# Six pairs of gate tiles computed in seven products instead of eight

## The chip, the cores and the metric

The kernel runs on one core of one Trainium2 chip. Its time is the device time of the execution in microseconds (us), as a median of three runs. A core has a matrix engine (TensorE, PE), three engines that work on rows of 128 partitions (VectorE or DVE, ScalarE or ACT, GpSimd or POOL), and DMA queues that load from memory; SyncE (SP) issues most of the loads. Each engine runs its own list of instructions in order, and semaphores make one wait for another.

## The reference

One layer of a decoder with four parallel branches (T = 512 steps, D = 1024 channels), shortened:

```python
h = rms_norm(x, mix_norm)
z = h @ w_in                                       # branches' inputs, and 4 x 1024 gate logits
y_sc, y_pool, y_conf, y_diff = ...                 # gated short conv, pooling, Conformer conv, differential attention
gates = sigmoid(gate_logits).reshape(b, s, 4, D)
merged = sum_i gates[i] * y[i]
x = x + merged @ w_o
x = x + conv_glu_ffn(rms_norm(x, ffn_norm), ffn_up, ffn_conv, ffn_down)

def conformer_conv(u, conv_w, conv_b, ln_g, ln_b, w_out):
    a, gate = split(u)
    y = causal_dwconv(a * sigmoid(gate), conv_w) + conv_b      # 31 taps, 512 channels
    y = silu(layer_norm(y, ln_g, ln_b))
    return y @ w_out
```

## The kernel before, in words

All activations lie with the channel on the partition and time along the row. Every matrix product is done in a reduced float format three times: weight and activation are both split into a high and a low part, and `mm3` (L181 to L184) issues high by high, high by low and low by high. A tile of the output is 128 channels by 512 steps and fills one of eight PSUM banks.

The weights come as a stream of chunks, 128 x 1024 each, in the order in which they are used. `fetch` loads a chunk into one of two raw buffers, `load_chunk` makes its high part on ScalarE (`wh`, L144) and its low part on VectorE (`wl`, L145); each has a ring of three buffers. A slot of the ring comes free when TensorE has used the chunk three places earlier.

TensorE goes through the stages in the order of the program: the Conformer's projections, q, k and v, the inputs of the short convolution and of pooling, and then for each branch the output projection and the gate of each of the eight tiles m: `ys`/`gts` (short convolution), `yp`/`gtp` (pooling), `yd`/`gtd` (attention). A gate tile is 8 x 3 matmuls of 512 columns on the normed input `hs`; `gate` applies the sigmoid on ScalarE, `merge` multiplies and adds on VectorE (L601, L607). The eight gates of the convolution branch (`gtc`) come next, and after them its output projection `yc`, `wo` and the feed-forward layer in two parts.

The 31 taps of the Conformer convolution for each of four channel tiles run on VectorE (`cacc`, L388 and L391) beside the matmuls of the attention, the short convolution and pooling. Between the c gates stands the layer norm: `norm_mean` (L632 to L637, ahead of gate m = 2) adds the four tiles to `cm`, splits the sum into `muh` (ScalarE) and `mul` (VectorE), and two matmuls with `ones` give the mean `mu`. The squares of the differences give `var` in the same way ahead of gate m = 4 (`norm_out`, L303 to L309), then SiLU makes the inputs of `yc`.

The last product of the feed-forward layer (`dn`) is done by a scheme with seven instead of eight block products: `seven` takes two tiles of the output and two blocks of the contraction, and multiplies sums of weight blocks with sums of activation blocks, 256 columns wide. The sums of the weights are made by DMA in memory, on the GpSimd queue (`make_sums`, L217 to L232), in 11 groups.

The order of ScalarE and VectorE is set at build time by a list scheduler that goes by its own costs; the order of GpSimd is that of the program.

Of the kernel before, what the change touches and what calls it, by code (L numbers as in the profile page):

```python
# [56 lines left out]
NTMP = 13  # L57
# [21 lines left out]
def hybrid_layer_kernel(ctx: ExitStack, tc: tile.TileContext, xT: bass.AP, w: bass.AP, cols: bass.AP, wa: bass.AP,  # L79
# [27 lines left out]
    up0 = w.shape[0] - 2 * NP  # L107
    plan = [("n", c) for c in range(up0 + 2 * CUT)]
    plan += [("s", c) for c in range(MP * CUT // 2)]
    plan += [("n", c) for c in range(up0 + 2 * CUT, w.shape[0])]  # L110
    plan += [("s", c) for c in range(MP * CUT // 2, MP * NP // 2)]
    sums = [dram.tile([P, GRP * SW], F32, name=f"sums{g}") for g in range(MP * NP // 2 // GRP)]
# [3 lines left out]
    def fetch(i, pieces=1):  # L116
        kind, c = plan[i]
        if kind == "s":
            g, o = divmod(c, GRP)
# [417 lines left out]
    def sc_in(j):  # L537
# [103 lines left out]
    def norm_out():  # L641
        rl = rsqrt(colsum(total, "var"), 1.0 / 512, t2("rl"), "rl")
        for j in range(4):
# [63 lines left out]
    def operands(i, ge, go, homes):  # L707
        def slot(name):
# [9 lines left out]
        nc.vector.scalar_tensor_tensor(  # L718
            out=wt[:, :H], in0=vt[:, :H], scalar=-1.0, in1=b22, op0=ALU.mult, op1=ALU.subtract)
        nc.vector.scalar_tensor_tensor(  # L720
            out=wt[:, H:], in0=wt[:, :H], scalar=-1.0, in1=b21, op0=ALU.mult, op1=ALU.subtract)
# [4 lines left out]
        return {"b11": (e[:, left], e[:, right]), "b22": pick(o, left), "b21": pick(o, right), "v1": pick(v, left),
                "t3": pick(v, right), "w2": pick(w_, left), "t4": pick(w_, right)}

    def seven(name, ops):
        a, b, c, d = (bank(f"{name}{x}") for x in "abcd")  # L730
        r1, r6, r2, r7, r5, r4, r3 = d[:, :H], a[:, :H], a[:, H:], b[:, :H], b[:, H:], c[:, :H], c[:, H:]
        n = len(ops)
        for k, x in enumerate(ops):
            a12, a11, a22, s3_, s1_, s2_, s4_ = blocks7()
            f, l = k == 0, k == n - 1
            mm3(r1, a11, x["b11"], f, l, True)
            mm3(r5, s1_, x["v1"], f, l, True)
            mm3(r6, s2_, x["w2"], f, l, True)
            mm3(r2, a12, x["b21"], False, l, True)
            mm3(r7, s3_, x["t3"], False, l, True)  # L740
            mm3(r4, a22, x["t4"], f, l, True)
            mm3(r3, s4_, x["b22"], False, l, True)
        s15 = t2(f"{name}s")
        s1_, s5_ = s15[:, :H], s15[:, H:]
        nc.scalar.copy(s1_, r1)
        nc.scalar.copy(s5_, r5)

        def two(x):
            return x.rearrange("p (b n) -> p b n", n=H)

        def twice(x):
            return x.unsqueeze(1).broadcast_to([P, 2, H])

        p1, p2, p3 = t2(f"{name}p"), t2(f"{name}q"), t2(f"{name}r")
        nc.vector.tensor_tensor(out=two(p1), in0=two(a), in1=twice(s1_), op=ALU.add)
        nc.vector.tensor_tensor(out=two(p2), in0=two(b), in1=twice(p1[:, :H]), op=ALU.add)
        nc.vector.tensor_tensor(out=p3, in0=c, in1=p2, op=ALU.add)
        nc.vector.tensor_tensor(out=s5_, in0=p2[:, :H], in1=s5_, op=ALU.add)
        return p1[:, H:], p3[:, H:], p3[:, :H], s5_

    parts = ((0, CUT), (CUT, NP))
    for part, (p0, p1) in enumerate(parts):
# [7 lines left out]
        for m in range(MP):  # L770
# [14 lines left out]
def _layout(x, mix_norm, w_in, sc_conv, sc_out, pool_w, pool_scale, conf_conv, conf_conv_b, conf_ln_g, conf_ln_b,  # L785
# [33 lines left out]
    for br, outs in ((0, so), (1, None), (3, do), (2, None)):  # L819
        for m in range(KD):  # L820
            if br == 2:
                tile_of(win, 36 + br * 8 + m)
                continue
            if outs is None:
                parts.append(pw[m // 2][:, (m % 2) * P:(m % 2 + 1) * P])
            else:
                tile_of(outs, m)
            tile_of(win, 36 + br * 8 + m)
# [65 lines left out]
```

## Time and profile before

| | |
|---|---|
| time, median of 3 runs | 880.69 us (880.65 to 880.88) |
| profiled execution | 880.71 us, of it 878.9 us in the span of the trace |
| granted TensorE clock, mean | 0.999 |
| busy, share of the span | PE 99%, PE weight loads 84%, DVE 75%, ACT 46%, POOL 8% |
| memory traffic | 182 GB/s over the span |

The span runs from the first to the last instruction. A busy share says how much of it an engine was at work; an engine with a low share can still be the one that is waited for in one place. Matmul records overlap, so their pace is read from one start to the next.

### The profile page before, as it was taken

The page shows a single profiled execution, that of the slowest core. Times are in us where ns is not written, and L with a number is a line of the kernel's source. Part 1 is how long each engine was busy: PE and PEld are TensorE (multiplying, and loading weights), DVE is VectorE, ACT ScalarE, POOL GpSimd, SP SyncE. Part 2 cuts the span into 40 slices and gives each one's busy share as a digit, 9 for nine tenths or more (in the row PEclk, how much of TensorE's full clock was granted, in tenths as well). Part 3 has the DMA queues.
Part 4 walks back from the last instruction along what each step waited for, and adds up shares of the span by engine and source line. Part 5 has one row for each costly group of instructions (what it writes and reads, how often), then busy time and mean ns, then how long its engine had stood idle before and what let it go on. Part 6 is the DMA issues. An engine that isn't in the chain of part 4 may idle for free.

```text
span 878.9 us, 11626 instructions
## 1 busy us (share of the span) xinstructions
PE 871.6 (99%) x4372; PEld 739.0 (84%) x4372; DVE 659.3 (75%) x1091; ACT 404.9 (46%) x636; POOL 71.3 (8%) x101
## 2 busy tenths in 40 slices
PE   9999999999999999999999999999999999999997
PEld 7888888888888888888888888888899888888997
DVE  7399966897957999534468566988886788888865
ACT  7343455464675432222564345444454344444542
POOL 1003300002411101111101100000000000000000
PEclk9999999999999999999999999999999999999999
DMA  6322242222479888888789862323662423334671
GB/s 235 114 96 97 80 123 73 72 97 97 138 200 213 183 215 206 220 216 205 189 208 250 226 157 72 119 97 103 208 178 63 131 98 97 96 106 158 174 210 49
DMA packets 54921, 128.98 MB, mean 147 GB/s; under 512 B 4896, under 2 KB 24352, under 8 KB 54688
## 3 DMA queue, kind: packets, MB, share of 16 engines
q1 hardware_dynamic: 36512, 95.98, 32.9%
q0 software_dynamic: 17776, 31.72, 18.5%
q8 instruction: 34, 0.56, 0.3%
q10 hardware_dynamic: 576, 0.53, 0.2%
q14 instruction: 23, 0.19, 0.1%
HBM read 126.12 MB, written 33.82 MB: 182 GB/s over the span
## 4 chain that ended last, share of the span: by engine, by line
PE 99%; DVE 0%; issue 0%; DVEq 0%
PE fg L182 5%; PE fu L182 5%; PE fg L183 5%; PE fu L183 5%; PE fg L184 5%; PE fu L184 5%; PE gts L182 2%; PE gts L184 2%; PE gts L183 2%; PE gtp L182 2%; PE gtc L182 2%; PE gtp L184 2%; PE gtc L183 2%; PE wo L183 2%; PE wo L182 2%; PE gtd L184 2%
## 5 line engine op out<-in xcount | busy, mean ns | idle before, releaser
L144 ACT CAST wh<-wr 128x1024 fp32r<-128x1024 f32 (+1 forms) x137 | 140.1, 1026 | 199.8 <-PE gtd L183 33.1
L145 DVE TENSOR_TENSOR wl<-wr,wh 128x1024 fp32r<-128x1024 f32 (+1 forms) x137 | 163.4, 1196 | 75.2 <-ACT wh L144 68.6
L391 DVE SCALAR_TENSOR_TENSOR cacc<-glu,colt,cacc 128x512 f32<-128x512 f32 x120 | 89.7, 752 | 1.9
L686 DVE SCALAR_TENSOR_TENSOR fc<-f,colt,fc 128x512 f32<-128x512 f32 x88 | 65.8, 749 | 7.7 <-ACT fc L684 6.4
L182 PE MATMUL fg<-hs,wh 128*128 128x512 f32 x176 | 68.5, 389 | 0.0
L184 PE MATMUL fg<-hs,wl 128*128 128x512 f32 x176 | 68.5, 389 | 0.0
L183 PE MATMUL fg<-hs,wh 128*128 128x512 f32 x176 | 68.5, 389 | 0.0
L182 PE MATMUL fu<-hs,wh 128*128 128x512 f32 x176 | 68.5, 389 | 0.0
L183 PE MATMUL fu<-hs,wh 128*128 128x512 f32 x176 | 68.5, 389 | 0.0
L184 PE MATMUL fu<-hs,wl 128*128 128x512 f32 x176 | 68.5, 389 | 0.0
L144 ACT CAST wh<-ra 128x384 fp32r<-128x384 f32 x44 | 22.6, 513 | 46.8 <-PE dn12c L183 7.6
L684 ACT ACTIVATE fc<-f,colt 128x512 f32<-128x512 f32 x44 | 31.6, 718 | 19.1 <-DVE f L103 16.6
L184 PEld LDWEIGHTS fu<-hs,wl 128*128 128x128 f32 x176 | 33.1, 188 | 6.9
L184 PEld LDWEIGHTS fg<-hs,wl 128*128 128x128 f32 x176 | 33.0, 188 | 6.9
L182 PEld LDWEIGHTS fg<-hs,wh 128*128 128x128 f32 x176 | 33.0, 188 | 6.9
L183 PEld LDWEIGHTS fg<-hs,wh 128*128 128x128 f32 x176 | 33.1, 188 | 6.8
L182 PEld LDWEIGHTS fu<-hs,wh 128*128 128x128 f32 x176 | 33.0, 188 | 6.8
L183 PEld LDWEIGHTS fu<-hs,wh 128*128 128x128 f32 x176 | 33.0, 188 | 6.8
L145 DVE TENSOR_TENSOR wl<-ra,wh 128x384 fp32r<-128x384 f32 x44 | 24.4, 554 | 19.1 <-ACT wh L144 19.0
L681 DVE TENSOR_TENSOR f<-fu,rs 128x512 f32<-128x512 f32 x22 | 15.1, 688 | 20.4 <-PE fu L184 20.4
L145 DVE TENSOR_TENSOR wl<-rb,wh 128x512 fp32r<-128x512 f32 x44 | 30.2, 687 | 0.0
L144 ACT CAST wh<-rb 128x512 fp32r<-128x512 f32 x44 | 27.1, 617 | 0.0
(1673 smaller groups left out, 2375.6 us busy)
## 6 DMA issues: line engine op xcount, KB each, us to landing
wr<-w SPq DMA_DIRECT2D x132, 512.0 KB, 3.3
sums<-s POOLq DMA_DIRECT2D x11, 1024.0 KB, 9.4
rb<-sums SPq DMA_DIRECT2D x44, 256.0 KB, 4.0
ra<-wa SPq DMA_DIRECT2D x44, 192.0 KB, 3.7
sums<-s POOLq DMA_DIRECT2D x11, 512.0 KB, 7.0
sums<-s POOLq DMA_DIRECT2D x11, 256.0 KB, 5.4
x<-xT SPq DMA_DIRECT2D x8, 256.0 KB, 5.6
xin<-xT SPq DMA_DIRECT2D x1, 1024.0 KB, 7.8
```

The lines of the kernel that those rows point to most:

```text
L144: nc.scalar.copy(hi[:, s], src)
L145: nc.vector.tensor_tensor(out=lo[:, s], in0=src, in1=hi[:, s].bitcast(F32), op=ALU.subtract)
L182: nc.tensor.matmul(ps, a[0], b[0], start=start, stop=False, skip_group_check=shared)
L183: nc.tensor.matmul(ps, a[0], b[1], start=False, stop=False, skip_group_check=shared)
L184: nc.tensor.matmul(ps, a[1], b[0], start=False, stop=stop, skip_group_check=shared)
L391: nc.vector.scalar_tensor_tensor(out=acc31[j], in0=glus[j][:, i:i + T], scalar=wc, in1=acc31[j], op0=ALU.mult, op1=ALU.add)
L681: nc.vector.tensor_tensor(out=u[:, 2:2 + T], in0=ps, in1=rs, op=ALU.mult)
L684: nc.scalar.activation(c, u[:, 2:2 + T], AF.Copy, scale=col("ffn_conv", o + 2))
L686: nc.vector.scalar_tensor_tensor(out=c, in0=u[:, i:i + T], scalar=col("ffn_conv", o + i), in1=c, op0=ALU.mult, op1=ALU.add)
```

## The change

Two pairs of gate tiles in the attention branch (m = 4, 5 and 6, 7) and all four pairs in the convolution branch go through `seven` as well. Their activation operands are sums of halves of `hs`, made once by `fold` on VectorE and ScalarE, four times. Their weights come in chunks of 128 x 896 (`wa` and sums made by DMA): four chunks for a pair. The sums now have 17 groups, the first three made early. All chunks, and the temporary of the fold, use one ring of raw buffers, which has three instead of two. `seven` issues the product r1 last in its first step. The splits of `yconf` go to the buffers of `od`.

```diff
@@ fetch, plan @@
+PLAN = [("n", 57 + 3 * STD // 2)]
+for _ in range((KD - STD) // 2):
+    PLAN += [("n", 1), ("s", FOLD)]
+PLAN += [("s", MP * FOLD), ("n", 4 + 8 + 2 * CUT), ("s", MP * CUT // 2), ("n", 2 * (NP - CUT)), ("s", MP * (NP - CUT) // 2)]
...
+        raw = wp.tile([P, CW], F32, tag="raw", name=f"wr{i}", bufs=3)
         if kind == "s":
             g, o = divmod(c, GRP)
-            ra, rb = m2(f"ra{i}", F32), m2(f"rb{i}", F32)
-            nc.sync.dma_start(ra[:, :AW], wa[c])
-            nc.sync.dma_start(rb, sums[g][:, o * SW:(o + 1) * SW])
-            return ((slice(0, AW), ra[:, :AW]), (slice(AW, AW + SW), rb))
-        raw = wp.tile([P, CW], F32, tag="raw", name=f"wr{i}", bufs=2)
+            n = AW + SW
+            nc.sync.dma_start(raw[:, :AW], wa[c])
+            nc.sync.dma_start(raw[:, AW:n], sums[g][:, o * SW:(o + 1) * SW])
+            return ((slice(0, n), raw[:, :n]),)
...
+    after(QLAG + 1, lambda: make_sums(0, EARLY))
...
-        u = padded(f"u{j}", 2)
+        u = padded(f"u{j}", 2, eng=nc.vector)
...
-    after(SUMU, make_sums)
+    after(SUMU, lambda: make_sums(EARLY, len(sums)))
...
+    def fold(i):
...
+        k = slice(2 * i, 2 * i + 2)
+        f = wp.tile([P, CW], F32, tag="raw", name=f"hf{i}", bufs=3)
+        nc.vector.tensor_tensor(
+            out=f.rearrange("p (k t) -> p k t", t=T), in0=hs[:, k, 0, :].bitcast(F32),
+            in1=hs[:, k, 1, :].bitcast(F32), op=ALU.add)
+        b12, b11, b22, b21 = (f[:, j * H:(j + 1) * H] for j in range(4))
+        vt, wt = t2(f"hv{i}"), t2(f"hw{i}")
+        nc.vector.tensor_tensor(
+            out=vt.rearrange("p (b n) -> p b n", n=H), in0=f[:, H:3 * H].rearrange("p (b n) -> p b n", n=H),
+            in1=b12.unsqueeze(1).broadcast_to([P, 2, H]), op=ALU.subtract)
+        combos(vt, wt, b11, b12, b21, b22)
+        v = split(vt, "", dst=(slot(f"hvh{i}"), slot(f"hvl{i}")))
+        w_ = split(wt, "", dst=(slot(f"hwh{i}"), slot(f"hwl{i}")))
...
+    def seven(name, ops):
...
+            if not f:
+                mm3(r1, a11, x["b11"], f, l, True)
+            mm3(r5, s1_, x["v1"], f, l, True)
...
+            mm3(r3, s4_, x["b22"], False, l, True)
+            if f:
+                mm3(r1, a11, x["b11"], f, l, True)
+        s15 = t2(f"{name}s")
+        s1_, s5_ = s15[:, :H], s15[:, H:]
+        nc.scalar.copy(s1_, r1)
+        nc.scalar.copy(s5_, r5)
...
+        nc.vector.tensor_tensor(out=two(p1), in0=two(a), in1=twice(s1_), op=ALU.add)
+        nc.vector.tensor_tensor(out=two(p2), in0=two(b), in1=twice(p1[:, :H]), op=ALU.add)
+        nc.vector.tensor_tensor(out=p3, in0=c, in1=p2, op=ALU.add)
+        nc.vector.tensor_tensor(out=s5_, in0=p2[:, :H], in1=s5_, op=ALU.add)
...
+    def gate_pair(m, name, keep=False):
+        c11, c12, n21, n22 = seven(f"g{name}{m}", hops)
+        gs = [m2(f"sg{name}{m + i}", F32) if keep else t2(f"sg{name}{m + i}") for i in range(2)]
+        for g, c, x, scale in (
+                (gs[0], right, c11, 1.0), (gs[0], left, c12, 1.0), (gs[1], right, n21, -1.0), (gs[1], left, n22, -1.0)):
+            nc.scalar.activation(g[:, c], x, AF.Sigmoid, scale=scale)
+        return gs
...
-    for m in range(KD):
+    for i in range(FOLD):
+        after(FOLDS * i, lambda i=i: fold(i))
+    for m in range(STD):
         py = mixed(m, "d", ydiff)
         merge(m, py, gate(m, "d"))
+    for m in range(STD, KD, 2):
+        pys = [mixed(m + i, "d", ydiff) for i in range(2)]
+        for i, g in enumerate(gate_pair(m, "d")):
+            merge(m + i, pys[i], g)
...
-            yconf.append(split(a, f"yc{j}"))
-
-    for m in range(KD):
+            yconf.append(split(a, "", dst=(od[0][:, j, :], od[1][:, j, :])))
+
+    for m in range(0, KD, 2):
         if m == 2:
             while events:
                 events.pop(0)[2]()
             norm_mean()
         if m == 4:
             norm_out()
-        gates.append(gate(m, "c", True))
+        gates += gate_pair(m, "c", True)
```

The built program shows what this moves. On TensorE, before the change, the two matmuls of the mean stand between two gates of 512 columns (`gtc`, tiles 1 and 2):

```order
L184 MATMUL gtc_3586<-hs,wl_3519 128x512
L322 MATMUL mu<-muh,ones 128x512
L323 MATMUL mu<-mul,ones 128x512
L182 MATMUL gtc_3659<-hs,wh_3555 128x512
L183 MATMUL gtc_3659<-hs,wh_3555 128x512
```

With the change, `gc0` and `gc2` are the first and second pair of c gates, and a to d their four banks:

```order
L189 MATMUL gc0c<-hs,wh_3810 128x256
L190 MATMUL gc0c<-hs,wh_3810 128x256
L191 MATMUL gc0c<-hs,wl_3811 128x256
L329 MATMUL mu<-muh,ones 128x512
L330 MATMUL mu<-mul,ones 128x512
L189 MATMUL gc2b<-at_111,wh_3839 128x256
L190 MATMUL gc2b<-at_111,wh_3839 128x256
```

The mean is still behind two tiles of gates, which are now one pair.

On VectorE, before the change, around the sums for the mean (`cm`, and `mul`, the low part of its split):

```order
L145 TENSOR_TENSOR wl_3519<-wr_3516,wh_3518 128x1024
L632 TENSOR_TENSOR cm<-cacc_705,cacc_1590 128x512
L601 TENSOR_TENSOR sgd_3548<-yd_3501,sgd_3548 128x512
L145 TENSOR_TENSOR wl_3556<-wr_3553,wh_3555 128x1024
L607 TENSOR_TENSOR acc_2764<-acc_2764,sgd_3548 128x512
L634 TENSOR_TENSOR cm<-cm,cacc_2626 128x512
L634 TENSOR_TENSOR cm<-cm,cacc_3285 128x512
L208 TENSOR_TENSOR mul<-cm,muh 128x512
```

With the change, on the same engine at the same place; `gc0p` to `gc0s` are the additions that end the first pair, `cacc_3367` is the Conformer's fourth channel tile:

```order
L667 TENSOR_TENSOR gc0q<-gc0b,gc0p 128x512
L398 SCALAR_TENSOR_TENSOR cacc_3367<-glu_208,colt,cacc_3367 128x512
L668 TENSOR_TENSOR gc0r<-gc0c,gc0q 128x512
L669 TENSOR_TENSOR gc0s<-gc0q,gc0s 128x256
L398 SCALAR_TENSOR_TENSOR cacc_3367<-glu_208,colt,cacc_3367 128x512
L727 TENSOR_TENSOR cm<-cacc_711,cacc_1608 128x512
L398 SCALAR_TENSOR_TENSOR cacc_3367<-glu_208,colt,cacc_3367 128x512
L729 TENSOR_TENSOR cm<-cm,cacc_2656 128x512
L398 SCALAR_TENSOR_TENSOR cacc_3367<-glu_208,colt,cacc_3367 128x512
L152 TENSOR_TENSOR wl_3955<-wr_3836,wh_3954 128x896
L729 TENSOR_TENSOR cm<-cm,cacc_3367 128x512
L215 TENSOR_TENSOR mul<-cm,muh 128x512
```

The last taps of the fourth tile and the end of the first c pair now stand ahead of `cm` and `mul`.

Where that fourth tile starts on VectorE: before the change, in the pooling branch, between the taps of the third tile (`cacc_2626`):

```order
L601 TENSOR_TENSOR acc_2764<-ys_2696,sgs_2762 128x512
L391 SCALAR_TENSOR_TENSOR cacc_2626<-glu_200,colt,cacc_2626 128x512
L388 TENSOR_SCALAR cacc_3285<-glu_202,colt 128x512
L391 SCALAR_TENSOR_TENSOR cacc_2626<-glu_200,colt,cacc_2626 128x512
L391 SCALAR_TENSOR_TENSOR cacc_3285<-glu_202,colt,cacc_3285 128x512
L391 SCALAR_TENSOR_TENSOR cacc_2626<-glu_200,colt,cacc_2626 128x512
L391 SCALAR_TENSOR_TENSOR cacc_3285<-glu_202,colt,cacc_3285 128x512
```

With the change, behind the low parts of the first 896-wide chunk and of the last fold, beside the first attention pair:

```order
L152 TENSOR_TENSOR wl_3393<-wr_3383,wh_3392 128x896
L215 TENSOR_TENSOR hwl_3364<-hw_3355,hwh_3363 128x512
L395 TENSOR_SCALAR cacc_3367<-glu_208,colt 128x512
L398 SCALAR_TENSOR_TENSOR cacc_3367<-glu_208,colt,cacc_3367 128x512 x5
L152 TENSOR_TENSOR wl_3431<-wr_3386,wh_3430 128x896
L690 TENSOR_TENSOR sgd_3421<-yd_3351,sgd_3421 128x512
L398 SCALAR_TENSOR_TENSOR cacc_3367<-glu_208,colt,cacc_3367 128x512
L696 TENSOR_TENSOR acc_2480<-acc_2480,sgd_3421 128x512
```

The first of its 31 instructions (L395, before the change L388) has moved from the pooling branch to the attention branch, behind the folds; the other 30 (L398, before L391) follow there.

## Rows read from the trace of the kernel before

**Rows 1.** Page, parts 1 and 4: busy us and share; last chain.

```profile
PE 871.6 (99%) x4372; PEld 739.0 (84%) x4372; DVE 659.3 (75%) x1091; ACT 404.9 (46%) x636; POOL 71.3 (8%) x101
...
PE 99%; DVE 0%; issue 0%; DVEq 0%
```

**Rows 2.** Stretches: length, busy us from PE to POOL, PEclk, DMA share, GB/s.

```profile
360.00:380.00 20.00, 20.00 (x90) 16.57 (x89) 6.59 (x8) 4.57 (x6) 1.61 (x2) 1.00 0.82 218
380.00:400.00 20.00, 20.00 (x90) 16.57 (x89) 8.87 (x10) 5.48 (x7) 2.98 (x4) 1.00 0.86 207
400.00:420.00 20.00, 20.00 (x90) 16.57 (x89) 9.07 (x12) 6.31 (x8) 2.88 (x4) 1.00 0.82 214
```

**Rows 3.** Timeline of VectorE: start, duration, line, operation, tiles.

```profile
355.25 0.74 DVE L391 SCALAR_TENSOR_TENSOR cacc<-glu,colt,cacc 128x512 f32<-128x512 f32 x1
...
415.64 0.69 DVE L607 TENSOR_TENSOR acc<-acc,sgd 128x512 f32<-128x512 f32 x1
416.24 1.41 DVE L634 TENSOR_TENSOR cm<-cm,cacc 128x512 f32<-128x512 f32 x2
418.34 0.69 DVE L208 TENSOR_TENSOR mul<-cm,muh 128x512 fp32r<-128x512 f32 x1 [0.68 <-ACT muh L207]
```

**Rows 4.** Timeline of TensorE at the mean.

```profile
423.23 0.39 PE L322 MATMUL mu<-muh,ones 128*128 128x512 f32 x1
```

**Rows 5.** Timeline of TensorE, start of yd4.

```profile
379.71 0.39 PE L182 MATMUL yd<-od,wh 128*128 128x512 f32 x1
379.94 0.39 PE L183 MATMUL yd<-od,wh 128*128 128x512 f32 x1
```

**Rows 6.** Timeline of TensorE in the seven products of dn.

```profile
650.43 0.28 PE L182 MATMUL dn01a<-at,wh 128*128 128x256 f32 x1
650.55 0.28 PE L183 MATMUL dn01a<-ol,wh 128*128 128x256 f32 x1
```

**Rows 7.** VectorE's lines, 340 to 480: busy us, mean ns, idle before.

```profile
L145 DVE TENSOR_TENSOR wl<-wr,wh 128x1024 fp32r<-128x1024 f32 x25 | 30.6, 1222 | 39.3 <-ACT wh L144 39.3
L391 DVE SCALAR_TENSOR_TENSOR cacc<-glu,colt,cacc 128x512 f32<-128x512 f32 x14 | 10.5, 750 | 0.3
```

**Rows 8.** Page, part 5: a low part 512 wide.

```profile
L145 DVE TENSOR_TENSOR wl<-rb,wh 128x512 fp32r<-128x512 f32 x44 | 30.2, 687 | 0.0
```

**Rows 9.** Additions ending seven: ns min/median/max, first and last start.

```profile
L755 DVE TENSOR_TENSOR dn01p<-dn01a,dn01s x1: 681/681/681, 655.9 to 655.9; 128x512 f32<-128x512 f32 x1
...
L758 DVE TENSOR_TENSOR dn01s<-dn01q,dn01s x1: 416/416/416, 658.2 to 658.2; 128x256 f32<-128x256 f32 x1
```

**Rows 10.** ScalarE's lines, 340 to 480.

```profile
L144 ACT CAST wh<-wr 128x1024 fp32r<-128x1024 f32 x26 | 27.4, 1052 | 59.5 <-PE gtd L183 33.1 <-PE gtc L183 13.9 <-PE yd L183 7.6
L646 ACT ACTIVATE cacc<-cacc,colt 128x512 f32<-128x512 f32 x4 | 3.1, 810 | 0.0
L304 ACT ACT_TABLE_LOAD x1 | 1.3, 1283 | 0.0
L207 ACT CAST muh<-cm 128x512 fp32r<-128x512 f32 x1 | 0.6, 618 | 3.8 <-DVE cm L634 3.8
```

**Rows 11.** Stretches at both ends of the span; the clock is PEclk.

```profile
0.00:4.00 4.00, 2.54 (x6) 2.07 (x7) 0.48 (x1) 1.58 (x2) 2.45 (x30) 1.00 0.43 139
...
873.00:874.00 1.00, 0.09 (x1) 0.00 (x0) 0.90 (x2) 0.00 (x0) 0.00 (x0) 1.00 0.00 0
876.00:877.00 1.00, 0.00 (x0) 0.00 (x0) 0.08 (x1) 0.00 (x0) 0.00 (x0) 0.86 1.03 345
```

**Rows 12.** Timeline of TensorE at the start.

```profile
1.46 4.64 PE L269 MATMUL warm<-zeros 128*128 128x512 f32 x10 [1.46 <-DVE zeros L266]
5.89 0.59 PE L182 MATMUL ca<-raw0h,wh 128*128 128x512 f32 x1
```

**Rows 13.** Loads, 300:480 and 560:620: KB each, us to landing.

```profile
wr<-w SPq DMA_DIRECT2D x33, 512.0 KB, 4.8
...
wr<-w SPq DMA_DIRECT2D x11, 512.0 KB, 3.3
```

More of the change, by code (lines that the diff above doesn't have):

```diff
@@ L47 @@
 SUMU = 30
+EARLY = 3
 DEEP = 2
+STD = 4
+FOLD = 4
+FOLDS = 12
+PLAN = [("n", 57 + 3 * STD // 2)]
+for _ in range((KD - STD) // 2):
+    PLAN += [("n", 1), ("s", FOLD)]
+PLAN += [("s", MP * FOLD), ("n", 4 + 8 + 2 * CUT), ("s", MP * CUT // 2), ("n", 2 * (NP - CUT)), ("s", MP * (NP - CUT) // 2)]
 LOG_EXP = "natural_log_exp_and_others"
@@ L56 @@
 SQ0 = 8
-NTMP = 13
+NTMP = 12
 SQS = 4
@@ L106, in hybrid_layer_kernel @@
     chunks = []
[L107 to L112, printed above, removed]
+    plan, n_of = [], {"n": 0, "s": 0}
+    for kind, n in PLAN:
+        plan += [(kind, n_of[kind] + i) for i in range(n)]
+        n_of[kind] += n
+    sums = [dram.tile([P, GRP * SW], F32, name=f"sums{g}") for g in range(n_of["s"] // GRP)]
     fetched = []
@@ L229, in make_sums @@
             lambda g: nc.gpsimd.dma_start(view(g, 3, 4), src(s3, g, 1), accum_op=ALU.add))
-        for g in range(len(sums)):
+        for g in range(g0, g1):
             for f in steps:
@@ L588, in hybrid_layer_kernel, with combos, table @@
     merged = []
-    after(SUMU, make_sums)
+    after(SUMU, lambda: make_sums(EARLY, len(sums)))
+    H = T // 2
+    left, right = slice(0, H), slice(H, T)
+    def combos(vt, wt, b11, b12, b21, b22):
+        nc.vector.scalar_tensor_tensor(
+            out=wt[:, :H], in0=vt[:, :H], scalar=-1.0, in1=b22, op0=ALU.mult, op1=ALU.subtract)
+        nc.vector.scalar_tensor_tensor(
+            out=wt[:, H:], in0=wt[:, :H], scalar=-1.0, in1=b21, op0=ALU.mult, op1=ALU.subtract)
+    def table(b11, b22, b21, v, w_):
+        pick = lambda x, c: (x[0][:, c], x[1][:, c])
+        return {"b11": b11, "b22": b22, "b21": b21, "v1": pick(v, left), "t3": pick(v, right),
+                "w2": pick(w_, left), "t4": pick(w_, right)}
@@ new lines, in hybrid_layer_kernel, with slot @@
+    hops = []
+    hhome = [x[:, i, :] for x in at_ for i in range(4)]
+    def fold(i):
+        def slot(name):
+            return hhome.pop(0) if hhome else m2(name)
+        k = slice(2 * i, 2 * i + 2)
[11 more added lines that the diff above has]
+        w_ = split(wt, "", dst=(slot(f"hwh{i}"), slot(f"hwl{i}")))
+        e, o = hs[:, 2 * i], hs[:, 2 * i + 1]
+        pick = lambda x, c: (x[:, 0, c], x[:, 1, c])
+        hops.append(table(pick(e, right), pick(o, left), pick(o, right), v, w_))
@@ L717, in operands @@
         nc.vector.tensor_tensor(out=vt[:, H:], in0=b22, in1=b12, op=ALU.subtract)
[L718 to L721, printed above, removed]
+        combos(vt, wt, b11, b12, b21, b22)
         v = split(vt, "", dst=(slot(f"vh{i}"), slot(f"vl{i}")))
         w_ = split(wt, "", dst=(slot(f"wh{i}"), slot(f"wl{i}")))
-        left, right = slice(0, H), slice(H, T)
         pick = lambda x, c: (x[0][:, c], x[1][:, c])
[L726 to L759, printed above, removed]
+        return table((e[:, left], e[:, right]), pick(o, left), pick(o, right), v, w_)
     parts = ((0, CUT), (CUT, NP))
@@ L818, in _layout, with gate_of @@
         tile_of(win, 12 + g)
[L819 to L828, printed above, removed]
+    def gate_of(br, m):
+        tile_of(win, 36 + br * 8 + m)
+    for m in range(KD):
+        tile_of(so, m)
+        gate_of(0, m)
+    for m in range(KD):
+        parts.append(pw[m // 2][:, (m % 2) * P:(m % 2 + 1) * P])
+        gate_of(1, m)
+    for m in range(STD):
+        tile_of(do, m)
+        gate_of(3, m)
+    for m in range(STD, KD):
+        tile_of(do, m)
     for m in range(KD):
```

29 lines of the change are left out of this document (23 added, 6 removed).

## The prediction

> **What bounds the kernel now.** I read the busy times first: TensorE is busy for 99% of the span, VectorE for 75%, and the chain that ended last is TensorE for 99% [rows 1]. So a matmul taken off shortens the kernel by its issue spacing, as long as TensorE is never kept waiting; whatever makes TensorE wait adds its full length. The question is therefore whether the covers still hold: the weight splits, and the two column sums of the Conformer's layer norm, `mu` and `var`, which TensorE meets in the middle of the c gates.
>
> The table of stretches comes next. VectorE is busy for only 6.59 us of 360 to 380, 8.87 of 380 to 400 and 9.07 of 400 to 420 [rows 2]. This idle time stands directly ahead of the c gates, and it is what let the mean be ready early: the last Conformer tap ran at 355.25, the last two `cm` sums from 416.24, `mul` at 418.34 to 419.03 [rows 3], and TensorE took `mu` at 423.23 [rows 4]. The cover was 4.2 us.
>
> **What the seven products give.** Matmuls of 512 columns start 0.227 us apart [rows 5], those of 256 columns 0.120 us apart [rows 6]. A pair of gates takes 2 x 8 x 3 = 48 wide matmuls, 48 x 0.2267 = 10.88 us; in seven products it takes 4 x 7 x 3 = 84 narrow ones, 84 x 0.1200 = 10.08 us. Six pairs save 6 x 0.80 = 4.8 us. That is all that TensorE can gain, and the kernel would then stand at 875.9.
>
> **What VectorE pays, and where.** The durations: a tap 0.750, a 1024-wide low part 1.22 [rows 7]; 512 wide 0.687 [rows 8]; a merge, which is 512 wide like `mul`, 0.69 [rows 3]. Where one doesn't need the result of the other they start some 0.09 us closer than they last: the merge at 415.64 lasts 0.69 us, and the next row starts 0.60 us later [rows 3]. A 896-wide low part therefore lies between 0.687 and 1.22; by the line through both it is 1.09, less 0.09, and I take 1.0. An epilogue of seven products is three additions 512 wide and one 256 wide, 3 x 0.68 + 0.42 = 2.5 us [rows 9].
>
> Each of the four folds is one addition 1024 wide, one subtraction 512 wide, two combinations 256 wide and two low parts: about 1.1 + 0.6 + 2 x 0.35 + 2 x 0.65 = 3.7 to 4.1 us, estimated from the same rows. The folds themselves hold no matmul up, since gd4 comes last of what follows them. But in the built order they take the place that the taps of j=3 had in the pool branch, and these 31 taps now stand beside the new gate pairs, right up to `cm`.
>
> I walk VectorE from the first of them. Ahead of it stands the low part of the first 896-wide chunk; its cast needs a slot of the ring of three, which TensorE frees at the end of yd3. In the rows, yd4 starts at 379.71 [rows 5]; 24 spacings before that is 374.27. With the cast (896 wide, between 0.62 and 1.05 us [rows 10]) and two low parts, the taps start at 376.9. From there to the end of `mul` VectorE has: 31 taps x 0.75 = 23.3; 14 low parts of 896 x 1.0 = 14.0; one of 1024, 1.1; ten merges x 0.65 = 6.5; three epilogues, 7.4; three `cm` sums, 2.0; the cast `muh` 0.62 [rows 10] and `mul` 0.69, 1.3. The sum is 55.6 us, so `mul` ends at 432.4.
>
> TensorE, from 379.71: two pairs of 5.44 + 10.08 bring it to 410.75, and gc0 ends at 420.83 if nothing waits. By the same list the low part of gc0's fourth chunk is ready 12.6 us before `mul`, at 419.9, while its third matmul is due at 418.55: **+1.4**. gc0 then ends at 422.2. TensorE takes its matmuls in order, and the two of `mu` stand directly behind gc0's last and ahead of gc2's first. It waits from 422.2 to 432.4: **+10.2**.
>
> Bounds of this wait. From below: even with VectorE free, gc0's epilogue, five taps, a low part, three sums and the split stand behind gc0's bank a, which is complete 1.08 us before gc0 ends. Epilogue 2.5 + 5 x 0.75 + 1.0 + 2.0 + 1.3 = 10.5, less 1.08 and some overlap, is 9.0 us. From above: if two late weight chunks hold VectorE up too, about 13.
>
> **What follows.** `var` stands behind gc2. Its `varh` is queued on ScalarE behind the cast of the chunk that reuses gc2's last slot and a sigmoid; its `varl` on VectorE behind that chunk's low part and the rest of gc2's epilogue. After gc2's end that is 0.9 + 0.4 + 0.6 = 1.9 us plus the latency of the handovers to `varh`, and 4.1 us to `varl`, of which eight narrow matmuls of gc4 cover 1.0: **+2.8** (1.9 to 4). Then ScalarE has two table loads of 1.28 us, four SiLU of 0.81 [rows 10], four casts and two copies ahead of the cast of gc6's third chunk. These 10.7 us begin 2.1 us before gc4's end, and the cast itself is done 7.7 us behind it at the earliest by overlapped starts; it is due after two chunks, 5.04 us: **+2.8** (1 to 4). From yc on, the order of every engine and its slack are as before; I cost that at nothing. The same goes for the other edits: TensorE's rows ahead of yd4 are those of before, the memset of `u` is four short writes, the splits of `yc` only land elsewhere, and moving the r1 product changes no count. Three early groups of sums are loads at a time when TensorE's weights come in with room; if they did delay a chunk there, 1 to 2 us would be lost.
>
> **The clock.** The granted clock was still 1.00 where the last matmul ended at about 873.1; in the stretch 876 to 877 it was 0.86 [rows 11], a mean over the two levels: 0.28 us of it at the lower, 1.2 GHz, so it fell at about 876.7. That was 3.6 us after the last matmul; I expect it to fall in a pause of 10 us and not in the short ones. The price of coming back is in the first matmuls: the ten `warm` ones, 512 wide, take from 1.46 to 5.89, where the next starts, 0.44 us each [rows 12], where 0.227 is the spacing later: 4.43 - 2.27 = **+2.2**. The clock column speaks against this, since it has 1.00 for 0 to 4 us too [rows 11]; by the column a restart costs nothing. I take the spacing, since it is what delays work.
>
> The Trainium skill, "TensorE: Matmul & The Clock Gate", Part 1 ("What's actually happening"), says that the throttled clock is the default state and that activity releases it; its note on trace caveats ("Seeing it yourself") says that the clock events of a trace are not always to be trusted. By that page the restart costs about what the spacing gives; by the column it costs 0, and the sum would be 2.2 us lower.
>
> **DMA.** A seven-product pair reads 1792 KB in place of 1024 KB. While the sums run a load of 512 KB lands after 4.8 us, against 3.3 us afterwards [rows 13]. Three raw slots, each held for about 5 us of landing and 2.1 us of splitting, give a chunk every 2.4 us against the 2.52 us that TensorE needs. This holds, but barely: I cost it at 0, with 4 as the upper end. Against a lasting shortage, TensorE's own pauses give the ring time to fill.
>
> **Sum**, against the profiled execution of 880.71 us (878.9 of span and 1.8 outside), which equals the median of 880.69: -4.8 + 1.4 + 10.2 + 2.8 + 2.8 + 2.2 = +14.6, so **895.3 us**.
>
> **Rivals.**
> 1. *The means arrive in time* (faster). If the taps of j=3 were run in the pool branch, or `mul` found a free VectorE, only the gain would be left: 875.9 us; it turns faster than before as soon as all waits together are under 4.8 us. For it: VectorE has 25 idle us between 360 and 400 [rows 2]. Against it: the taps are behind a slot that TensorE frees, the list from there is 55.6 us long, and even its last part alone is 9 us. 3 in 100; about no change, 2 in 100.
> 2. *Only the shortest wait for `mu`*: 9.0 - 4.8 and nothing further, or 2 to 3 us of the rest: 885 to 889. For it: handovers overlap more than I count, and ScalarE may run ahead. Against it: `var` is tied to gc2's end. 15 in 100.
> 3. *The late chunks decide as well*: mul at +13, contention +4 on top: 899 to 903. For it: the landing row under the sums. Against it: the pauses themselves. 15 in 100.
> 4. *The clock does not fall or comes back at once*: 893.1, within my range. 20 in 100 of the forecast's own cases.
>
> My forecast, 889 to 899 about 895.3, has 65 in 100. The range, which should hold 8 in 10, is 887 to 901. Differences under 0.2% (1.8 us) count as no change. Faster 0.03, same 0.02, slower 0.95.
>
> **What would show it.** In the profile after, TensorE's busy share is down, and its longest wait, some 10 us, is for `mul`, between gc0 and gc2; taps of line 398 run until just before it. VectorE has no pause from about 377 to 432. The spacing within the new pairs is 0.120 us, except for the first microseconds behind `mu`, where it is about twice that. There are shorter waits for `varh` and `varl`, and for gc6's third chunk. If `mu` waits for less than 5 us, my list of VectorE's work is wrong; if new waits stand before 410 or behind yc, supply and not order is the cause. If the pairs themselves take over 10.1 us with no wait, the gain was mis-sized.

## The result, and the profile after

The changed kernel takes 905.64 us (median of four, 900.72 to 908.5), the kernel before 880.67 on the same chip: ratio 1.0277 (95% interval 1.0232 to 1.0322). That is slower, as forecast, but by 25.0 us where 14.6 had been predicted, and beyond the range's upper end of 901. The profiled execution (905.76) has a span of 903.9 us, 25.0 more than before; every stage below is read from it.

The page now has TensorE busy for 97% and the last chain no longer on TensorE alone (parts 1 and 4; compare [rows 1]):

```profile
PE 874.7 (97%) x4588; PEld 750.9 (83%) x4588; DVE 694.2 (77%) x1111; ACT 420.3 (46%) x636; POOL 92.9 (10%) x121
...
PE 90%; DVE 4%; DMA 3%; ACT 2%; issue 1%; SPq 0%; DVEq 0%; ACTq 0%
```

TensorE's waits say where (what waited, for what; us in total, times, longest):

```profile
PE mu L329 <- ACT muh L214: 10.3, 1, 10.3
PE var L329 <- ACT varh L214: 5.6, 1, 5.6
PE gc6d L189 <- ACT wh L151: 2.8, 1, 2.8
PE gc0d L191 <- DVE wl L152: 1.4, 1, 1.4
PE gd6d L191 <- DVE wl L152: 0.6, 1, 0.6
PE gc0d L189 <- DVE gd6p L666: 0.5, 1, 0.5
PE gc0c L189 <- ACT gd6s L656: 0.4, 1, 0.4
```

The starts of the stages give each one's length (TensorE's timeline; start and duration in us):

```profile
385.84 0.28 PE L189 MATMUL gd4b<-at,wh 128*128 128x256 f32 x1
...
395.92 0.40 PE L189 MATMUL yd<-od,wh 128*128 128x512 f32 x1
...
401.38 0.28 PE L189 MATMUL gd6b<-at,wh 128*128 128x256 f32 x1
...
412.74 0.28 PE L189 MATMUL gc0b<-at,wh 128*128 128x256 f32 x1
...
436.33 0.79 PE L329 MATMUL mu<-muh,ones 128*128 128x512 f32 x1 [10.30 <-ACT muh L214]
...
454.98 0.80 PE L329 MATMUL var<-varh,ones 128*128 128x512 f32 x1 [5.59 <-ACT varh L214]
...
467.02 0.28 PE L189 MATMUL gc6b<-at,wh 128*128 128x256 f32 x1
...
481.62 0.40 PE L189 MATMUL yc<-od,wh 128*128 128x512 f32 x1
```

The line of yd is the first of yd6, so gd4 took 10.08 us: the gain per pair is as worked out. gd6 took 11.36 and gc0 13.29 (412.74 to the wait at 426.03). `mu` was then taken 13.1 us later than before [rows 4]. `mu` and gc2 took 13.06 us for 10.53 of work (two matmuls of 0.227 and a pair of 10.08), `var` and gc4 12.04 for 10.53, gc6 14.60 with its wait of 2.77. yc began 24.7 us later than before (456.88), and that distance stayed to the end.

The clock explains the stretches without a listed wait (length; busy us of PE, PEld, DVE, ACT, POOL; PEclk, DMA share, GB/s; compare [rows 11]):

```profile
436.00:438.00 2.00, 1.67 (x4) 1.14 (x5) 0.81 (x2) 0.27 (x1) 1.03 (x1) 0.50 0.80 247
442.00:444.00 2.00, 2.00 (x19) 2.00 (x18) 1.65 (x2) 0.74 (x1) 1.01 (x2) 1.00 0.04 6
475.00:476.00 1.00, 1.00 (x5) 1.00 (x6) 1.00 (x1) 1.00 (x4) 0.44 (x1) 0.61 0.32 30
476.00:478.00 2.00, 2.00 (x12) 2.00 (x11) 1.33 (x3) 1.64 (x2) 0.00 (x0) 0.50 2.53 640
```

It was at 1.2 GHz (0.50) behind `mu`, behind `var`, and even behind gc6's wait of 2.8 us, where by this column TensorE had already resumed when it fell.

VectorE around `mul` (timeline; compare [rows 3]):

```profile
430.75 0.74 DVE L398 SCALAR_TENSOR_TENSOR cacc<-glu,colt,cacc 128x512 f32<-128x512 f32 x1
431.41 0.68 DVE L727 TENSOR_TENSOR cm<-cacc,cacc 128x512 f32<-128x512 f32 x1
432.01 0.74 DVE L398 SCALAR_TENSOR_TENSOR cacc<-glu,colt,cacc 128x512 f32<-128x512 f32 x1
432.68 0.68 DVE L729 TENSOR_TENSOR cm<-cm,cacc 128x512 f32<-128x512 f32 x1
433.28 0.74 DVE L398 SCALAR_TENSOR_TENSOR cacc<-glu,colt,cacc 128x512 f32<-128x512 f32 x1
433.94 1.08 DVE L152 TENSOR_TENSOR wl<-wr,wh 128x896 fp32r<-128x896 f32 x1
434.94 0.68 DVE L729 TENSOR_TENSOR cm<-cm,cacc 128x512 f32<-128x512 f32 x1
436.31 0.69 DVE L215 TENSOR_TENSOR mul<-cm,muh 128x512 fp32r<-128x512 f32 x1 [0.68 <-ACT muh L214]
```

These are the rows of the built order, one behind the other. VectorE did pause further ahead, though: between 376 and 437 it waited four times for casts, 5.6 us in all.

```profile
DVE wl L152 <- ACT wh L151: 5.6, 4, 2.4
```

The wait for `var` has another origin; the chain of waits, in order of time (start, length, what):

```profile
444.57 8.49 DMA wr<-sums
453.16 0.94 ACT wh L151
454.10 0.32 ACT sgc L677
454.42 0.52 ACT varh L214
454.98 0.80 PE var L329
```

A chunk's second load took 8.5 us. Its cast stands ahead of `varh` on ScalarE, so the split for the variance waited for a weight chunk of the pair behind `var`: gc4's third, counted by the order of the casts.

### The profile page after: what moved, and what is told of

It is laid out like the page before. It is cut to its first block, busy times and chain, and to the rows that moved or that the text cites. A ratio compares the mean times of both kernels' runs of the same rounds, so it can differ in the third digit from the quotient of the medians.

```text
span 903.9 us, 12229 instructions
## 1 busy us (share of the span) xinstructions
PE 874.7 (97%) x4588; PEld 750.9 (83%) x4588; DVE 694.2 (77%) x1111; ACT 420.3 (46%) x636; POOL 92.9 (10%) x121
## 4 chain that ended last, share of the span: by engine, by line
PE 90%; DVE 4%; DMA 3%; ACT 2%; issue 1%; SPq 0%; DVEq 0%; ACTq 0%
PE fg L190 4%; PE fu L190 4%; PE fg L191 4%; PE fg L189 4%; PE fu L191 4%; PE fu L189 4%; DMA wr<-sums 3%; PE gts L189 2%; PE gts L191 2%; PE gts L190 2%; PE wo L191 2%; PE gtp L189 2%; PE gtp L191 2%; PE wo L190 2%; PE wo L189 2%; PE gtp L190 2%
## 5 line engine op out<-in xcount | busy, mean ns | idle before, releaser
L151 ACT CAST wh<-wr 128x1024 fp32r<-128x1024 f32 (+3 forms) x193 | 191.3, 994 | 249.3 <-issue 29.5
L152 DVE TENSOR_TENSOR wl<-wr,wh 128x1024 fp32r<-128x1024 f32 (+3 forms) x193 | 223.3, 1160 | 80.4 <-ACT wh L151 71.8
L398 DVE SCALAR_TENSOR_TENSOR cacc<-glu,colt,cacc 128x512 f32<-128x512 f32 x120 | 89.7, 748 | 2.1
L235 POOL DMA_DIRECT2D sums<-s x17 | 17.2, 1015 | 167.1 <-DMA sums<-s 167.1
L776 DVE TENSOR_TENSOR f<-fu,rs 128x512 f32<-128x512 f32 x22 | 15.1, 688 | 20.3 <-PE fu L191 20.3
L234 POOL DMA_DIRECT2D sums<-s x17 | 17.4, 1024 | 117.1 <-DMA sums<-s 117.1
L236 POOL DMA_DIRECT2D sums<-s x17 | 17.2, 1012 | 108.9 <-DMA sums<-s 103.5
L498 ACT ACTIVATE p<-p,st 128x128 f32<-128x128 f32 (+3 forms) x32 | 17.7, 555 | 16.9 <-DVE st L495 16.8
## 6 DMA issues: line engine op xcount, KB each, us to landing
sums<-s POOLq DMA_DIRECT2D x17, 1024.0 KB, 10.1
```

Source lines behind the costliest of these rows:

```text
L151: nc.scalar.copy(hi[:, s], src)
L152: nc.vector.tensor_tensor(out=lo[:, s], in0=src, in1=hi[:, s].bitcast(F32), op=ALU.subtract)
L234: lambda g: nc.gpsimd.dma_start(sums[g], s1[g], accum_op=ALU.add, max_dma_last_dim=GRP * SW),
L235: lambda g: nc.gpsimd.dma_start(view(g, 2, 4), src(s2, g, 2), accum_op=ALU.add),
L236: lambda g: nc.gpsimd.dma_start(view(g, 3, 4), src(s3, g, 1), accum_op=ALU.add))
L398: nc.vector.scalar_tensor_tensor(out=acc31[j], in0=glus[j][:, i:i + T], scalar=wc, in1=acc31[j], op0=ALU.mult, op1=ALU.add)
```

## The experiments

**Taps earlier.** One number in the changed kernel.

```diff
-TAP1 = 560
+TAP1 = 460
```

> One number is changed in the changed kernel: the 31 taps of each channel tile are spread over 460 instead of 560 units of the program, so that VectorE's list has the taps of j=3 ahead of the gate pairs and none between the end of gc0 and mul. Theory A (the wait for mu is VectorE's order): the wait falls from 10.3 us by the five taps of 0.75 us that stood in it, to about 6 us, since gc0's epilogue, one low part, the sums cm and the split stay ahead of mul; the two waits for low parts in gd6 and gc0 (0.6 and 1.4) go; the clock still falls in the pause. About 899 us. Theory B (TensorE waits because weight loads land late while the sums run, whatever VectorE's order): mu still waits about 10 us, and the time stays at 903 to 908.

Measured: 905.78 us (899.87 to 907.69). A miss for the expectation of A. The wait for `mu` fell only to 9.2 us, and the scores ahead of the branches now waited for VectorE:

```profile
PE mu L329 <- ACT muh L214: 9.2, 1, 9.2
PE var L329 <- ACT varh L214: 5.7, 1, 5.7
PE gc6d L189 <- ACT wh L151: 2.8, 1, 2.8
PE sc L487 <- DVE acc L690: 2.4, 1, 2.4
```

VectorE had pauses ahead of `mul` and was still late: two low parts in its list waited 2.2 and 1.2 us for their casts, with loads of up to 8.7 us behind these. The pooling branch began 5.8 us later than in the kernel before. The waits in gd6 and gc0 did go, as A expected; but the second loads of gd6's chunks landed in 3.4 to 5.9 us here, against 4.7 to 10.7 in the changed kernel, so this run doesn't say which of the two took them away. So order alone doesn't set the time: with the taps out of the way, late loads hold the same list.

**Sums later.** Groups 6 to 16 held behind the last c gate.

```diff
+GATES = 6
...
-    after(SUMU, lambda: make_sums(EARLY, len(sums)))
+    after(SUMU, lambda: make_sums(EARLY, GATES))
...
+    hold = const.tile([P, 1], F32, name="hold")
+    nc.gpsimd.tensor_copy(out=hold, in_=gates[-1][:, :1])
+    make_sums(GATES, len(sums))
```

> Of the changed kernel only the time of the later sum groups is moved: groups 6 to 16, which the feed-forward layer needs, are issued once the last c gate is there (a one-column copy on GpSimd that reads it holds the queue), so that no sums run beside the d and c pairs except their own, which are done by then. Theory A (order) leaves the wait for mu at 10 us and the wait for gc6 at 2.8. Theory B (late loads) says that the weight loads of the pairs land in 3 to 4 us instead of 6, the waits in gd6 and gc0 shrink by 1 to 2 us and var's from 5.6 to about 2.8, what the order of ScalarE and VectorE alone gives. Both together: about 899 us. If the moved sums now delay wo or the feed-forward layer, 1 to 3 us come back. If late loads do not matter, 904 to 907.

Measured: 907.12 us (904.08 to 908.28), against about 899 expected; but yc began at 471.83, 9.8 us earlier than in the changed kernel, and no wait is left in gd6 or gc0:

```profile
PE mu L330 <- ACT muh L215: 8.5, 1, 8.5
PE gc6d L190 <- ACT wh L152: 2.8, 1, 2.8
PE dn03d L192 <- DVE wl L153: 2.5, 2, 1.9
PE var L330 <- ACT varh L215: 1.7, 1, 1.7
```

The loads of the pairs (KB each, us to landing, 385 to 450), in the changed kernel 6.9 and 4.9 us, now landed in:

```profile
wr<-sums SPq DMA_DIRECT2D x18, 256.0 KB, 3.4
wr<-wa SPq DMA_DIRECT2D x18, 192.0 KB, 2.5
```

The gain was given back in the feed-forward layer: dn0 began 15.0 us behind the kernel before, and the second part's seven products 25.0 us behind.

**Sums later, in part** (groups 9 to 16 held).

> The changed kernel with sum groups 3 to 8 made as before and only groups 9 to 16 held until the last c gate; VectorE's order, the taps and the norm stay. In the run with all later sums held, the d and c stages gained 9.8 us (yc began at 471.8 instead of 481.6) and the seven products of the feed-forward layer, which then ran beside the sums, lost about as much. Theory B (seven products beside sums wait for late loads, wherever they stand) says: yc again at 472 to 474, and nearly no loss in dn0, as its five groups are done in time: 895 to 898 us. If the loss in dn0 came from something else, the time stays at 904 to 907.

Measured: 901.78, above the 895 to 898 expected. yc began at 472.0 as expected, but dn0 still lost 5 us (15.2 us behind at its start, 20.3 at the second part's): the held groups ran until 684, and dn0 began at 646.6.

**TensorE kept busy in the two pauses.**

```diff
         ps = bank(name)
+        for _ in range({"mu": 40, "var": 20}.get(name, 0)):
+            nc.tensor.matmul(ps, ones, hs[:, 0, 0, :], start=True, stop=True)
         nc.tensor.matmul(ps, ones, a[0], start=True, stop=False)
```

> The changed kernel with matmuls that do nothing for the result: 40 of 512 columns (9.1 us) into the bank of mu ahead of its two matmuls, and 20 (4.5 us) ahead of those of var, so that TensorE is busy in most of these two pauses. Theory A (the first products after a pause are slow because the clock fell): the granted clock stays at 1.00 there, gc2 takes 10.1 us instead of 11.7 and gc4 10.1 to 10.5 instead of 11.5, mu's and var's own matmuls are back to 0.23 us each; some 4 us less than the changed kernel, about 901.5. Rival (they are slow because weights or banks come late, and the clock column is only a sign): gc2 and gc4 stay at 11.5 or more and the time stays at 904 to 907.

Measured: 901.63 (901.3 to 902.48), 4.0 less than the changed kernel by the medians. One execution of the changed kernel took only 900.72, so the stages are the firmer evidence. The clock stayed up:

```profile
438.00:440.00 2.00, 1.58 (x9) 1.22 (x10) 1.12 (x2) 0.26 (x1) 0.00 (x0) 1.00 0.34 108
440.00:444.00 4.00, 4.00 (x36) 4.00 (x35) 3.90 (x7) 3.23 (x5) 1.02 (x1) 1.00 0.80 155
```

gc4 took 10.07 us (455.40 to 465.47) instead of 11.45, gc2 10.67 instead of 11.74, where 10.1 had been expected. So the slow products behind a pause are the clock's, not the weights', but for 0.6 us of gc2.

**Taps, norm and sums together.** The taps over 460 units, groups 6 to 16 held, and the norm's splits issued a pair earlier than their matmuls:

```diff
-        if m == 2:
+        if m == 0:
             while events:
                 events.pop(0)[2]()
             norm_mean()
+        if m == 2:
+            norm_var()
         if m == 4:
             norm_out()
```

`norm_mean` now ends with the split into `muh` and `mul`; `norm_var` holds the matmuls of `mu`, the differences, the squares and the split of `var`; `norm_out` begins with the matmuls of `var`.

> Taps over 460 units, the later sums after the last c gate, and the norm's steps in another place of the program: the sums cm and the split into muh and mul ahead of the first c pair, the split of var ahead of the second pair's epilogue, with the matmuls of mu and var where they were. If order and late loads are the whole of the loss, no wait for mu or var is over 1 us, the clock stays up until gc6, only gc6's wait for ScalarE (up to 2.8 us and a restart of 1.8) is left: 877 to 882 us. If VectorE or ScalarE has too much to do in these stages whatever the order, waits of 3 us and more come up elsewhere: 885 or more.

Measured: 897.39 (895.09 to 899.98). The waits for `mu` and `var` went nearly as expected (1.4 us left, for `mu`), and yc began 4.6 us behind the kernel before. 4.2 of these were there when the pooling branch began, behind the early taps, and dn0, beside the held sums, lost another 9.7. So the expected 877 to 882 was wrong on these two, and the taps' place has a price on either side.

Two runs with the norm placed in this way, groups 9 to 16 held and the taps over 540 and 520 units:

> Groups 9 to 16 held until the last c gate, the norm's splits placed ahead of the c pairs as in the run called best, and the taps over 540 units instead of 460, so that most of those of j=3 run between pooling and the first pair, where VectorE had pauses. Theory A with B: no loss in the pooling branch (the run with 460 units lost some 4.5 us there), mu and var wait for under 2 us together, yc at 455 to 459, dn0 as in the kernel before: 877 to 884 us. If VectorE simply has too little room for 24 us of taps and 16 us of folds, mu waits for 3 us or more, or the pooling branch loses 3: 885 to 890.

> As the run with 540 units, with the taps over 520. Theory A with B: the taps are done some 5 us earlier, which takes mu's wait to nothing but may cost the pooling branch 1 to 3 us: 878 to 885 us. If the taps' place does not matter in this stretch, the same time as with 540 within 1 us.

Measured: 891.91 and 890.89. yc was 1.8 and 1.4 us behind; the loss in dn0 (8.7 and 8.6 us) made both miss.

**No sums beside dn0** (norm as above, taps over 520; groups 9 to 13 behind the last c gate, 14 to 16 behind dn0).

> The run with taps over 520 units (890.9 us) had lost only 1.2 us to the kernel before when dn0 began, and 8.6 more between the start of dn0 and the second half of the feed-forward layer. Here groups 9 to 13 are made after the last c gate and groups 14 to 16 only after dn0, so that none runs beside dn0. Theory B (seven products beside sums wait for late loads): the 8.6 go, 881.5 to 884 us. If the loss in dn0 has another cause (the raw ring, the new order of r1), it stays: 889 to 892.

Measured: 882.01, ratio 1.0020 (1.0009 to 1.0031). dn0 lost nothing (0.8 us behind at its start and at the second part's).

**The kernel before with sums beside dn0.**

```diff
-    after(SUMU, make_sums)
+    after(SUMU, lambda: make_sums(0, 5))
...
+        if part == 0:
+            hold = const.tile([P, 1], F32, name="hold")
+            nc.gpsimd.tensor_copy(out=hold, in_=ops[-1]["v1"][0][:, :1].bitcast(F32))
+            make_sums(5, len(sums))
         for m in range(MP):
             c11, c12, n21, n22 = seven(f"dn{part}{m}", ops)
```

> The kernel before, with one thing moved: the last six groups of the weight sums, which only the second part of the feed-forward layer needs, are issued when dn0 begins instead of in one go with the others. Nothing else changes. Theory B: dn0, which loads 448 KB for every 2.5 us as the changed kernel's gate pairs do, now runs beside sums and waits for late loads: 5 to 10 us more between the start of dn0 and that of the second part, 886 to 891 us, with everything ahead of it as before. If two raw rows and a read-ahead of two are enough beside sums, the time stays at 880.7 within 1 us.

Measured: 881.11, ratio 1.0001 (0.9992 to 1.0010): no loss. The loads of dn0 did land late (632 to 695):

```profile
rb<-sums SPq DMA_DIRECT2D x12, 256.0 KB, 8.6
ra<-wa SPq DMA_DIRECT2D x12, 192.0 KB, 6.2
```

later than in the changed kernel's pairs, and TensorE didn't wait. Theory B in this form falls: late loads cost nothing there. The kernel before has tiles of its own for these chunks, and up to four were under way at once here; in the changed kernel they share three raw buffers with all other chunks and the folds, and at most three were under way beside the pairs (385 to 450).

**Five raw buffers**, and nothing else but four tiles fewer of another kind (`MID`), which make the room.

```diff
-MID = 35
+MID = 31
...
-        raw = wp.tile([P, CW], F32, tag="raw", name=f"wr{i}", bufs=3)
+        raw = wp.tile([P, CW], F32, tag="raw", name=f"wr{i}", bufs=5)
...
-        f = wp.tile([P, CW], F32, tag="raw", name=f"hf{i}", bufs=3)
+        f = wp.tile([P, CW], F32, tag="raw", name=f"hf{i}", bufs=5)
```

> The changed kernel with five raw buffers instead of three (room from four fewer tiles in the pool of 512-wide ones); order, taps, norm and sums as they are. The kernel before with its sums moved beside dn0 lost nothing, although its loads landed in 6 to 9 us there: its chunks had buffers of their own and could be asked for further ahead. Theory C (loads are late under the sums, and the ring of three cannot cover it): with five, the waits in gd6 and gc0 (2.9 us, of which 1.4 may be VectorE's) go, and var's falls from 5.6 to about 2; mu's stays at 8.5 to 10 by order: 894 to 898 us. If the memory cannot deliver 178 GB/s beside the sums whatever is in flight, 903 to 907.

Measured: 896.74 (896.35 to 897.18), 8.9 less, and the waits of the run with held sums:

```profile
PE mu L329 <- ACT muh L214: 8.5, 1, 8.5
PE gc6d L189 <- ACT wh L151: 2.8, 1, 2.8
PE var L329 <- ACT varh L214: 1.7, 1, 1.7
```

although the loads landed as late as in the changed kernel (385 to 450):

```profile
wr<-sums SPq DMA_DIRECT2D x18, 256.0 KB, 6.5
wr<-wa SPq DMA_DIRECT2D x18, 192.0 KB, 5.3
```

What the two buffers buy is an earlier request, not more loads at once: here too at most three chunks were under way. In the changed kernel eleven chunks in a row, from gd6's first to gc2's third, were cast within 0.4 us of their landing; with five buffers each of the 24 chunks of the pairs lay ready for at least 2.1 us. The second load of gc4's third chunk was issued at 426.8 instead of 444.6.

**Five raw buffers with the new order** (taps over 520, norm as above, no group held):

> Taps over 520 units and the norm's steps as in b_520, with five raw buffers, and no sum group held back at all: all run as in the changed kernel. With the later groups held in two places the same order took 882.0. Theory C: the deeper ring replaces the holds, 881 to 884 us. If contention costs more than the ring covers: 886 or more, with waits for casts and low parts in the pairs.

Measured: 882.43, within what the theory of the ring gave. Two more buffers replace both holds: they cover the sums beside the pairs, and as no group is held, all are done at 605.7, ahead of dn0 at 632.6. Sums beside dn0 with five buffers were not tried.

**The norm a pair earlier still**, on top of the version without sums beside dn0:

> As c1, with every step of the norm one pair earlier: the split of mu ahead of the end of the second d pair, mu's matmuls ahead of gc0, var's ahead of gc2, so that the SiLUs are done before gc6. If ScalarE's queue of SiLUs, splits and table loads is what held gc6's and yc's casts (waits of 1.4 and 2.5 us, and the clock behind them), these go: 877 to 880 us, faster than the kernel before. If the four more table loads of 1.3 us that this order has hold other casts up instead: 882 to 887.

Measured: 890.34, above both cases of the expectation. ScalarE now changed its tables back and forth between the logarithm and the gates' sigmoids, and its row of SiLUs stood ahead of gc4's casts; TensorE waited 2.1 us in gc2 and 4.3 in gc4, the latter with the clock down behind it. The waits moved rather than went.

**Four buffers for high and low parts**, splits three chunks ahead, on top of the same version:

```diff
-MID = 35
+MID = 31
...
-AHEAD = 2
+AHEAD = 3
...
-        hi = wp.tile([P, CW], F32R, tag="whi", name=f"wh{c}", bufs=3)
-        lo = wp.tile([P, CW], F32R, tag="wlo", name=f"wl{c}", bufs=3)
+        hi = wp.tile([P, CW], F32R, tag="whi", name=f"wh{c}", bufs=4)
+        lo = wp.tile([P, CW], F32R, tag="wlo", name=f"wl{c}", bufs=4)
```

> As c1 (882.0 us), with four buffers for the high and low parts instead of three and the splits asked for three chunks ahead instead of two, so that the cast of yc's first chunk stands ahead of the SiLUs on ScalarE. What is left of the loss in c1 are waits of 1.4 us in gc6 and 1.8 ahead of yc's second product, and 1 to 2 us of low clock behind them. If ScalarE's 8 us of SiLUs, splits and table loads are their cause, these go: 877 to 880, faster than the kernel before by 0.1 to 0.4%. If the waits move on to the next chunk: 881 to 883.

Measured: 879.59 (ten runs, 879.17 to 880.08) against 881.14, ratio 0.9983 (0.9973 to 0.9992): 1.6 us under the kernel before. The interval separates this from no difference, but it is less than the 0.2% that the prediction counted as a change. Of all waits behind the first microseconds one is left:

```profile
PE mu L330 <- ACT muh L215: 1.5, 1, 1.5
```

The cast of yc's first chunk (1024 wide) now stands ahead of the table load and the SiLUs on ScalarE:

```profile
447.80 1.03 ACT L152 CAST wh<-wr 128x1024 fp32r<-128x1024 f32 x1
448.85 1.28 ACT L748 ACT_TABLE_LOAD   x1
450.15 1.52 ACT L748 ACTIVATE cacc<-cacc,colt 128x512 f32<-128x512 f32 x2
```

## Why the prediction was wrong

The mechanism, the direction and the largest term held; the range failed on two steps: late chunks, costed at nothing, which show in the rows for the low parts and `var`, and the clock, sized too small. Term by term, in us:

| term | predicted | measured |
|---|---|---|
| six pairs in seven products | -4.8 | -4.8, if all six are like gd4 (-0.80), which ran undisturbed |
| low parts in gd6 and gc0 | +1.4 | +4.5 (gd6 +1.3, gc0 +3.2; 1.4 is the wait named) |
| `mu` | +10.2 | +10.3 |
| `var` | +2.8 | +5.6 |
| gc6 | +2.8 | +2.8 |
| clock | +2.2 | +5.8 (2.5 behind `mu`, 1.5 behind `var`, 1.8 in gc6) |
| ahead of yd4 | 0 | +0.7 |

These add up to 24.9 of the 25.0.

The 0.7 ahead of yd4 is no effect of the change that the record shows: 0.6 of it was there when the projection to q began, at 52.14 us against 51.55 before, and in the runs with sums held, whose program is the same up to that point, it began at 51.16 and 51.19.

**The step that failed** is the paragraph on DMA: "Three raw slots, each held for about 5 us of landing and 2.1 us of splitting, give a chunk every 2.4 us against the 2.52 us that TensorE needs. This holds, but barely: I cost it at 0, with 4 as the upper end." The landing used was the median of one load [rows 13]; a chunk here is two, and while the sums ran its second part took 6.9 us in the median and up to 10.7. With 6.9 the same division gives a chunk every 3.0 us, so it does not hold. Holding the sums back, and equally five raw buffers under the same late loads, took the waits in gd6 and gc0 away and brought `var` from 5.6 to 1.7, and the time in the latter to 896.7. That is 1.4 us from what had been forecast, which is in part luck: the waits there are 4.2 us shorter than forecast (`mu` 8.5 for 10.2, `var` 1.7 for 2.8, low parts 0 for 1.4), and the clock and the rest make up 5.6. The prediction's own sign of short supply, a new wait ahead of 410, came true: TensorE waited in gd6 until 407.8. The case priced for late chunks, 899 to 903, had the right cause but mostly the wrong place: it put them ahead of `mul`, where they cost 1.8 us (10.3 against 8.5), and they struck `var` with 3.9.

**The clock** was priced once, with "I expect it to fall in a pause of 10 us and not in the short ones". It fell in all three, even behind 2.8 us. The price of one restart, 2.2 from the spacing of the `warm` matmuls, was about right for the first (2.5). The column that had 1.00 at the start of the span speaks correctly of it here (0.50 behind `mu`), and with matmuls in the two pauses gc2 and gc4 were 1.1 and 1.4 us shorter: spacing and column agree in this trace, and the spacing is what had to be trusted at the start.

**What held.** The wait for `mu` comes mostly from the order of VectorE's list; without late chunks it is 8.5 us, just under the lower bound of 9.0. That 10.2 was met to 0.1 us is luck. The working had it as the sum of durations alone, 55.6 us without a pause; measured were 58.9 us from the first tap (378.10) to the end of `mul` (437.00), of which 5.6 are waits for casts, and gc0 ended 3.8 us later than worked out. TensorE resumed at `muh`, 0.7 us ahead of the end of `mul`, to which the working had counted. The run with early taps shows the same list waiting for loads, so its two causes cover each other: taking away one of them left 9.2 or 8.5 us. Only the norm's splits placed ahead of the first c pair, with the taps early enough, took it to 1.5.

**The rivals.** That the means come in time is out. So is that only the shortest wait for `mu` is left: it was 10.3, and all the others came too. That the clock comes back at once is out by the run with fillers. What stays open is why the time of the changed kernel spreads over 8 us while that with five buffers stays within 1; late loads differing from run to run would do that, but no run here was made to show it.

## What to carry to other kernels

A pause is priced with everything that it drags along: the wait, the slow matmuls behind it, and each later wait that hangs on its end. A ring's depth is checked by the slowest load that shares the memory at that time, for all parts of a chunk; a median of one load taken elsewhere says little, and loads of 6 to 9 us cost nothing here where they were asked for early enough. And a short instruction that TensorE needs is issued in the program ahead of the epilogue that would otherwise stand before it in an in-order queue.

## What had not been expected of the hardware

By the clock column, the clock can fall after TensorE has resumed: in gc6 a pause of 2.8 us ended at 474.99, the granted clock was 1.00 until some 0.2 us later, averaged 0.61 over 475 to 476 and 0.50 over 476 to 478, and the pair took 1.8 us more. The length of the pause alone doesn't decide: with five raw buffers the clock fell behind a wait of 1.7 us for `var`, which ended at 446.14, and with the norm a pair earlier it stayed at 1.00 over 432 to 436, in and behind the wait of 2.1 us in gc2.

```profile
446.00:448.00 2.00, 1.86 (x9) 1.82 (x10) 1.92 (x4) 1.07 (x4) 0.17 (x1) 0.63 1.02 339
448.00:450.00 2.00, 2.00 (x10) 1.90 (x10) 0.00 (x0) 1.22 (x3) 1.37 (x2) 0.52 0.94 249
```

The Trainium skill, "TensorE: Matmul & The Clock Gate", Part 1 ("A second HAM failure mode: psum-queue depth-cycling"), describes a kernel in which TensorE idles briefly between groups of matmuls, the clock goes back and forth, and a re-throttle and re-warm cost is paid between bursts. This trace shows such a cost behind a single short pause, 1.8 us, and nothing of a pause in every iteration.
